# A mixture-of-experts dispatch on one core: the first group's last store in two pieces, and a load that waits for the first of them

## The chip, the cores and the metric

The kernel runs on one core of a Trainium2 chip. The metric is the device time of one execution in microseconds; three runs of the kernel before took 239.73, 239.82 and 239.9 us, so the median is 239.82 us.

## The reference

16384 tokens each have 512 numbers (`x`) and 8 router logits. For each token the two largest softmax probabilities are taken and divided by their sum, and the token's row is written twice, once scaled by each of the two weights, the smaller one first.

```python
logits_max = np.max(router_logits, axis=-1, keepdims=True)
probs = np.exp(router_logits - logits_max)
probs = probs / np.sum(probs, axis=-1, keepdims=True)
topk_indices = np.argsort(probs, axis=-1)[..., -k:]
topk_probs = np.take_along_axis(probs, topk_indices, axis=-1)
topk_probs = topk_probs / np.sum(topk_probs, axis=-1, keepdims=True)
x_expanded = x[:, :, np.newaxis, :].repeat(k, axis=2)
return (x_expanded * topk_probs[..., np.newaxis]).astype(np.float32)
```

Everything is float32. `x` is 33.6 MB, the logits 0.5 MB, and the output, with two rows for each token, 67.1 MB.

## The kernel before

The weights of the two chosen experts depend only on the difference of the two largest logits, so `top2_weights` finds these two with a small tree of maxima and minima on VectorE (lines 26 to 36) and gets both weights from two sigmoids on ScalarE (lines 37 and 38). They land in the tile `WA`.

The tokens are worked in two groups of 8192. In a group each of the 128 partitions holds 64 consecutive tokens, called rows below. A group has two loads of 32 rows each (line 118), into rows 0 to 31 and 32 to 63 of the tile `xs`, which both groups share. It then has four steps of 16 rows. Each step multiplies 16 rows by their two weights, which makes 32 output rows, and stores them (lines 131 to 159). The output goes in turn to the tile `osp` (steps 1 and 3) and back over rows of `xs` that have been used up: step 2 writes rows 0 to 31 of `xs`, step 4 rows 32 to 63. The product is a `tensor_tensor` on VectorE (line 147); of each group's first step a few rows go to ScalarE (line 140).

Every load and store of `x` and of the output is one transfer of 128 partitions x 16384 float32, so 64 KB for a partition and 8.4 MB in all. All transfers are issued by the SP engine, in program order (`tc.keep_in_program_order`), on one hardware queue. The order is: first load, logits, second load, four stores of the first group; third and fourth load; four stores of the second group. A transfer whose data is not ready, or whose target is still in use, holds up SP and all issues behind it.

Around the place of the change the order is this. The first group's second store (rows 0 to 31 of `xs`) must have landed before the second group's first load may overwrite those rows. The first group's last store reads rows 32 to 63 of `xs`, and the second group's second load, which overwrites them, waits for its landing. The second group's first load has nothing to do with the last store's data: it is issued right behind it and stands behind it in the queue. After that, the second group's first multiplication (line 147, into `osp`) waits for that load, and the second group's first store (line 158) waits for the multiplication.

Of the kernel before, what the change touches and what calls it, by code (L numbers as in the profile page):

```python
# [1 line left out]

# [4 lines left out]

F32 = mybir.dt.float32
ALU = mybir.AluOpType
ACTF = mybir.ActivationFunctionType  # L10
P = 128


def top2_weights(nc, WA, dlt, room, logits, E):

    tt = nc.vector.tensor_tensor
    hi, lo, n = None, None, E  # L20
    while n > 1:
        n //= 2
        if hi is None:
            a, b = logits[:, :, 0:n], logits[:, :, n : 2 * n]
            nhi, nlo = room(n), b
            tt(nhi, a, b, op=ALU.max)  # L26
            tt(nlo, a, b, op=ALU.min)  # L27
        else:
            a, b = hi[:, :, 0:n], hi[:, :, n : 2 * n]
            nhi, nlo, tmp = room(n), room(n), room(n)  # L30
            tt(tmp, lo[:, :, 0:n], lo[:, :, n : 2 * n], op=ALU.max)  # L31
            tt(nlo, a, b, op=ALU.min)  # L32
            tt(nlo, nlo, tmp, op=ALU.max)  # L33
            tt(nhi, a, b, op=ALU.max)  # L34
        hi, lo = nhi, nlo
    tt(dlt, hi[:, :, 0], lo[:, :, 0], op=ALU.subtract)  # L36
    nc.scalar.activation(WA[:, :, 0], dlt, ACTF.Sigmoid, scale=-1.0)  # L37
    nc.scalar.activation(WA[:, :, 1], dlt, ACTF.Sigmoid, scale=1.0)  # L38

GROUPS = [64, 64]

LOADS = [[32, 32], [32, 32]]
BASE = [0, 0]

STORES = [
    [(0, 16, "osp", 2), (16, 16, "xs", 0), (32, 16, "osp", 0), (48, 16, "xs", 32)],
    [(0, 16, "osp", 2), (16, 16, "xs", 0), (32, 16, "osp", 0), (48, 16, "xs", 32)],
]  # L50

L = 18

FREE = [2, 2]

ACT_ROWS = [5, 1]


@with_exitstack
def kernel(  # L60
    ctx: ExitStack,
    tc: tile.TileContext,
    x: bass.AP,
    router_logits: bass.AP,
    k: bass.AP,
    out: bass.AP,
):
    nc = tc.nc
    B, S, D = x.shape
    E = router_logits.shape[-1]  # L70
    N = B * S
    assert int(k) == 2 and E == 8 and N == P * sum(GROUPS)
    M = N // P

    x_v, o_v = [], []
    t0 = 0
    for n in GROUPS:
        t1 = t0 + P * n
        x_v.append(
            x.rearrange("b s d -> (b s) d")[t0:t1].rearrange("(p m) d -> p m d", p=P)  # L80
        )
        o_v.append(
            out.rearrange("b s k d -> (b s) k d")[t0:t1].rearrange(
                "(p m) k d -> p m k d", p=P
            )
        )
        t0 = t1

    wpool = ctx.enter_context(tc.tile_pool(name="wpool", bufs=1))
    xs = wpool.tile([P, max(GROUPS), D], F32)  # L90
    osp = wpool.tile([P, L, 2, D], F32)
    WA = wpool.tile([P, M, 2], F32)
    dlt = wpool.tile([P, M], F32)


    flat = osp.rearrange("p l k d -> p (l k d)")
    taken = [0]

    def room(n):
        o = taken[0]  # L100
        taken[0] += M * n
        return flat[:, o : o + M * n].rearrange("p (m n) -> p m n", n=n)

    logits = room(E)

    def place(where, at, n):

        if where == "osp":
            return osp[:, at : at + n]
        return xs[:, at : at + 2 * n, :].rearrange("p (r k) d -> p r k d", k=2)  # L110

    m0 = 0
    stores = []
    for g, G in enumerate(GROUPS):
        x0, r = BASE[g], 0
        for n in LOADS[g]:

            load = nc.sync.dma_start(xs[:, x0 + r : x0 + r + n, :], x_v[g][:, r : r + n, :])  # L118
            tc.keep_in_program_order(load)
            r += n  # L120
            if g == 0 and r == 32:
                n0 = GROUPS[0]
                assert GROUPS[1] == n0
                both = router_logits.rearrange("b s e -> (b s) e").rearrange(
                    "(g p m) e -> p g (m e)", g=2, p=P
                )
                at = logits.rearrange("p (g m) e -> p g (m e)", g=2)
                tc.keep_in_program_order(nc.sync.dma_start(at, both))
                top2_weights(nc, WA, dlt, room, logits, E)
        assert r == G  # L130
        for r, n, where, at in STORES[g]:
            og = place(where, at, n)

            again = where == "osp" and at == 0 and r > 0
            cuts = [0, FREE[g], n] if again else [0, n]
            if r == 0:
                cuts = [0, n - ACT_ROWS[g]]
                for j in range(n - ACT_ROWS[g], n):
                    for k2 in range(2):
                        nc.scalar.activation(  # L140
                            og[:, j, k2, :],
                            xs[:, x0 + r + j, :],
                            ACTF.Copy,
                            scale=WA[:, m0 + r + j, k2 : k2 + 1],
                        )
            for a, b in zip(cuts, cuts[1:]):
                nc.vector.tensor_tensor(  # L147
                    og[:, a:b],
                    xs[:, x0 + r + a : x0 + r + b, :]
                    .unsqueeze(2)  # L150
                    .to_broadcast([P, b - a, 2, D]),
                    WA[:, m0 + r + a : m0 + r + b, :]
                    .unsqueeze(3)
                    .to_broadcast([P, b - a, 2, D]),
                    op=ALU.mult,
                )

            stores.append(nc.sync.dma_start(o_v[g][:, r : r + n], og))  # L158
            tc.keep_in_program_order(stores[-1])
        m0 += G  # L160


# [1 line left out]
_INS = ['x', 'router_logits', 'k']  # L164
_OUTS = [((16, 1024, 2, 512), 'float32')]

_NUMBERS = {'k': 2}


# [26 lines left out]
```

## Time and profile before

The profile is that of one execution, which took 239.97 us; its span, from the first instruction to the last, is 238.2 us.

| What | Value |
|---|---|
| median of 3 runs | 239.82 us |
| the profiled execution | 239.97 us |
| its span | 238.2 us |
| ScalarE (ACT) busy | 9.3 us |
| GpSimd (POOL) busy | 0.2 us |
| mean rate of the transfers | 425 GB/s |
| read from and written to device memory | 34.08 MB and 67.11 MB |

How to read it: an engine's busy time counts its instructions and not its waits. The DMA row divides the span into 40 equal slices (5.96 us each) and gives the mean busy share of the 16 DMA engines in tenths. The chain of waits starts at the last instruction and goes back, at each step, to whatever released it; shown in order of time, each piece has its start, its length and what it was. `SPq` is SP's issuing of a transfer, and a piece that begins with `DMA` runs from the issue of a transfer to its landing, that is, until its data are in place and the semaphore that others wait for has been raised. Such a piece includes the time the transfer stood in the queue behind others.

### The profile page before, as it was taken

The page shows a single profiled execution, that of the slowest core. Times are in us where ns is not written, and L with a number is a line of the kernel's source. Part 1 is how long each engine was busy: PE and PEld are TensorE (multiplying, and loading weights), DVE is VectorE, ACT ScalarE, POOL GpSimd, SP SyncE. Part 2 cuts the span into 40 slices and gives each one's busy share as a digit, 9 for nine tenths or more (in the row PEclk, how much of TensorE's full clock was granted, in tenths as well). Part 3 has the DMA queues.
Part 4 walks back from the last instruction along what each step waited for, and adds up shares of the span by engine and source line. Part 5 has one row for each costly group of instructions (what it writes and reads, how often), then busy time and mean ns, then how long its engine had stood idle before and what let it go on. Part 6 is the DMA issues. An engine that isn't in the chain of part 4 may idle for free.

```text
span 238.2 us, 110 instructions
## 1 busy us (share of the span) xinstructions
DVE 135.4 (57%) x21; ACT 9.3 (4%) x15; POOL 0.2 (0%) x4
## 2 busy tenths in 40 slices
DVE  0000899999599999000000039999958999950000
ACT  2000370000000000000000020000000000000000
POOL 0000000000000000000000000000000000000000
DMA  9899898989999998989899998989898989899894
GB/s 352 363 517 440 352 528 352 528 352 484 396 440 440 396 484 352 528 352 528 352 484 396 396 484 352 528 352 517 363 517 363 517 363 495 385 462 418 374 506 176
DMA packets 2000, 101.19 MB, mean 425 GB/s; under 512 B 208, under 2 KB 208, under 8 KB 464
## 3 DMA queue, kind: packets, MB, share of 16 engines
q1 hardware_dynamic: 2000, 101.19, 98.6%
HBM read 34.08 MB, written 67.11 MB: 425 GB/s over the span
## 4 chain that ended last, share of the span: by engine, by line
DMA 47%; DVE 41%; issue 0%; SPq 0%; ACT 0%; DVEq 0%
DVE osp L147 24%; DMA xs<-in_x_dram 19%; DMA out_dram<-osp 19%; DVE xs L147 14%; DMA osp<-in_router_logits_dram 10%; DVE osp L26 0%; DVE osp L27 0%; DVE osp L33 0%; DVE osp L34 0%; DVE osp L32 0%; DVE osp L31 0%; SPq L118 0%; SPq L158 0%; ACT WA L38 0%; DVE dlt L36 0%
## 5 line engine op out<-in xcount | busy, mean ns | idle before, releaser
L147 DVE TENSOR_TENSOR osp<-xs,WA 128x2048 f32<-128x2048 f32 (+3 forms) x6 | 62.8, 10468 | 52.1 <-DMA xs<-in_x_dram 45.6
L147 DVE TENSOR_TENSOR xs<-xs,WA 128x16384 f32<-128x16384 f32 x4 | 68.9, 17225 | 0.3
L26 DVE TENSOR_TENSOR osp<-osp 128x512 f32<-128x512 f32 x1 | 0.7, 693 | 23.8 <-DMA osp<-in_router_logits_dram 23.8
L140 ACT ACTIVATE osp<-xs,WA 128x512 f32<-128x512 f32 x12 | 7.6, 707 | 106.1 <-DMA xs<-in_x_dram 106.1
L37 ACT ACTIVATE WA<-dlt 128x128 f32<-128x128 f32 x1 | 0.3, 315 | 25.8 <-DVE dlt L36 25.8
L37 ACT ACT_TABLE_LOAD x1 | 1.3, 1283 | 0.7 <-PEq L177 0.7
L27 DVE TENSOR_TENSOR osp<-osp 128x512 f32<-128x512 f32 x1 | 0.7, 691 | 0.0
L32 DVE TENSOR_TENSOR osp<-osp 128x256 f32<-128x256 f32 (+1 forms) x2 | 0.7, 352 | 0.0
L34 DVE TENSOR_TENSOR osp<-osp 128x256 f32<-128x256 f32 (+1 forms) x2 | 0.7, 352 | 0.0
L31 DVE TENSOR_TENSOR osp<-osp 128x256 f32<-128x256 f32 (+1 forms) x2 | 0.7, 351 | 0.0
L33 DVE TENSOR_TENSOR osp<-osp 128x256 f32<-128x256 f32 (+1 forms) x2 | 0.7, 350 | 0.0
L36 DVE TENSOR_TENSOR dlt<-osp 128x128 f32<-128x128 f32 x1 | 0.3, 293 | 0.0
L38 ACT ACTIVATE WA<-dlt 128x128 f32<-128x128 f32 x1 | 0.3, 297 | 0.0
L177 POOL MEMSET const-bfloat16-1.0<- 128x1 bf16 x1 | 0.1, 101 | 0.0
L177 POOL MEMSET const-uint8-127<- 128x1 uint8 x1 | 0.1, 101 | 0.0
L177 POOL MEMSET const-float32-0.0<- 128x1 f32 x1 | 0.1, 98 | 0.2 <-issue 0.2
L177 POOL MEMSET const-float32-1.0<- 128x1 f32 x1 | 0.1, 98 | 0.0
## 6 DMA issues: line engine op xcount, KB each, us to landing
osp<-in_router_logits_dram SPq DMA_DIRECT2D x1, 512.0 KB, 22.7
xs<-in_x_dram SPq DMA_DIRECT2D x4, 40.3
out_dram<-osp SPq DMA_DIRECT2D x4, 23.0
out_dram<-xs SPq DMA_DIRECT2D x4, 25.0
```

The lines of the kernel that those rows point to most:

```text
L26: tt(nhi, a, b, op=ALU.max)
L27: tt(nlo, a, b, op=ALU.min)
L31: tt(tmp, lo[:, :, 0:n], lo[:, :, n : 2 * n], op=ALU.max)
L32: tt(nlo, a, b, op=ALU.min)
L33: tt(nlo, nlo, tmp, op=ALU.max)
L34: tt(nhi, a, b, op=ALU.max)
L36: tt(dlt, hi[:, :, 0], lo[:, :, 0], op=ALU.subtract)
L37: nc.scalar.activation(WA[:, :, 0], dlt, ACTF.Sigmoid, scale=-1.0)
L38: nc.scalar.activation(WA[:, :, 1], dlt, ACTF.Sigmoid, scale=1.0)
L140: nc.scalar.activation(og[:, j, k2, :], xs[:, x0 + r + j, :], ACTF.Copy, scale=WA[:, m0 + r + j, k2 : k2 + 1],)
L147: nc.vector.tensor_tensor(og[:, a:b], xs[:, x0 + r + a : x0 + r + b, :] .unsqueeze(2) .to_broadcast([P, b - a, 2, D]), WA[:, m0 + r + a : ...
L177: nc = _bacc.Bacc("TRN2", target_bir_lowering=False, num_devices=1)
```

## The change

The last store of the first group is issued as two transfers, of partitions 0 to 111 and of partitions 112 to 127, one right after the other. The list `stores` then has one more entry, so that when the second group's first load is issued, `stores[-2]` is the one of 112 partitions. This load gets a wait of its own for that store's landing; the second group's second load, which overwrites the data of both, waits for the 16 partitions' landing, too. The instructions of the compute engines and their order are the same as before; SP has one issue more.

```diff
@@ -116,6 +116,15 @@
         for n in LOADS[g]:
 
             load = nc.sync.dma_start(xs[:, x0 + r : x0 + r + n, :], x_v[g][:, r : r + n, :])
+            if g == 1 and r == 0:
+                tc.add_manual_dep(
+                    load.ins,
+                    stores[-2].ins.name,
+                    mybir.DependencyInfo(
+                        mybir.DependencyClass.Sync, mybir.DependencyReason.DATA
+                    ),
+                    reason="begin when the store ahead of the last has landed",
+                )
             tc.keep_in_program_order(load)
             r += n
             if g == 0 and r == 32:
@@ -155,8 +164,10 @@
                     op=ALU.mult,
                 )
 
-            stores.append(nc.sync.dma_start(o_v[g][:, r : r + n], og))
-            tc.keep_in_program_order(stores[-1])
+            last = g == 0 and r + n == G
+            for p0, p1 in [(0, P - 16), (P - 16, P)] if last else [(0, P)]:
+                stores.append(nc.sync.dma_start(o_v[g][p0:p1, r : r + n], og[p0:p1]))
+                tc.keep_in_program_order(stores[-1])
         m0 += G
```

## The prediction

> **What bounds the kernel now.** I began with the page: its span, the busy row of the engines, the two DMA rows and the queue.
>
> ```profile
> span 238.2 us, 110 instructions
> DVE 135.4 (57%) x21; ACT 9.3 (4%) x15; POOL 0.2 (0%) x4
> DMA  9899898989999998989899998989898989899894
> DMA packets 2000, 101.19 MB, mean 425 GB/s; under 512 B 208, under 2 KB 208, under 8 KB 464
> q1 hardware_dynamic: 2000, 101.19, 98.6%
> ```
>
> The compute engines are idle for 43% of the span or more, while the 16 DMA engines are busy for 98.6% of it and the DMA row has no empty slice. This kernel is a stream of transfers, and only a gap in the stream, or a slower packet, can move its time. The packets say how the stream is built: 2000 less 464 small ones leaves 1536 large ones; over the 12 transfers of x and out that is 128 each, one per partition, or 8 on each of 16 engines (64 KB apiece, since a transfer is 128 x 16384 float32).
>
> Next the chain of waits in order of time, for where the stream sits around the edit.
>
> ```profile
> 40.30 22.22 DMA out_dram<-osp
> ...
> 94.92 0.33 SPq L158
> 95.26 0.05 issue
> 95.31 45.13 DMA xs<-in_x_dram
> 140.44 0.03 issue
> ...
> 140.53 16.17 DVE osp L147
> ...
> 156.76 22.46 DMA out_dram<-osp
> ```
>
> The second piece is the edit's place. The first group's last store (I call the stores S1 to S8 and the x loads L1 to L4) is S4, issued at 94.92. L3 is issued at 95.31, right behind it in the same queue, and lands 45.13 us later, at 140.44. It spends most of that time behind S3 and S4. Then the timeline and the issue table, asked for one issue at a time, give the landings.
>
> ```profile
> 57.56 0.34 SPq L158 DMA_DIRECT2D out_dram<-xs  x1
> ...
> 77.67 0.33 SPq L158 DMA_DIRECT2D out_dram<-osp  x1
> ...
> 120.88 0.34 SPq L118 DMA_DIRECT2D xs<-in_x_dram  x1
> ```
>
> ```profile
> out_dram<-xs SPq DMA_DIRECT2D x1, 24.3
> ...
> out_dram<-osp SPq DMA_DIRECT2D x1, 23.5
> ...
> out_dram<-xs SPq DMA_DIRECT2D x1, 25.9
> ...
> xs<-in_x_dram SPq DMA_DIRECT2D x1, 39.0
> ```
>
> The last column is us from issue to landing; the rows are S2, S3, S4 and L4. S1 landed at 40.30 + 22.22 = 62.52, S2 at 81.86, S3 at 77.67 + 23.5 = 101.17, S4 at 94.92 + 25.9 = 120.82, L4 at 159.9. So a store takes (101.17 - 62.52) / 2 = 19.33 us in the undisturbed stream, and one partition's packet 19.33 / 8 = 2.42 us. L4 took 159.9 - 140.44 = 19.46. Loads and stores go at one pace, so its limit is neither the read nor the write of the far memory but what both use: the 16 engines, or the way from each engine into on-chip memory. The trace cannot part these two, and the forecast hangs on which it is.
>
> From S3's landing to L3's is 140.44 - 101.17 = 39.27 us against 2 x 19.33 = 38.66: the switch from storing to loading loses 0.6 us. That is all there is to win here.
>
> **The change, part by part.** One more issue on SP: 0.33 us (the S4 row above), at about 95.3. S3 occupies the engines until 101.17, so some 6 us of queued work hide it; without that cover it would cost its 0.33 us. The small packets are 13 issues x 16 = 208 under 512 B, so 16 more come with the new store; S1 to S3 ran at 19.33 us with theirs included, and I cost them at nothing.
>
> The added wait. L3 no longer stands in the queue from 95.31 but is issued when the 112 partitions have landed. Behind it on SP stand L4, which waited for S4 anyway, and S5, which is not due before 156.76.
>
> ```profile
> SPq L118 <- DMA out_dram<-xs: 24.3, 1, 24.3
> ...
> DVE osp L147 <- DMA xs<-in_x_dram: 45.6, 1, 45.6
> ```
>
> The first row is L4's wait for S4; it now begins later and costs nothing by itself. The second is VectorE waiting for L3, and whatever delays L3 is added to it in full. What a load needs when nothing is queued ahead is seen once, in L1:
>
> ```profile
> xs<-in_x_dram SPq DMA_DIRECT2D x1, 21.8
> ```
>
> That is 21.8 - 19.33 = 2.5 us of start and landing beyond the bare transfer. The cover for it is the 16-partition store, one packet on each engine. Spread evenly at the known pace that is 2.42 us: the wait would be hidden to within 0.1 us. If the cover were gone, the wait would cost up to 2.5 us.
>
> The split store is the expensive part, and the trace has no transfer on fewer than 128 partitions. The nearest in size is the logits load:
>
> ```profile
> 1.15 22.67 DMA osp<-in_router_logits_dram
> ```
>
> It landed at 23.82, 1.3 us behind L1 (0.72 + 21.8 = 22.52), which is 0.5 MB at about the stream's pace; but it too covers all 128 partitions. So I bound the 16 partitions (1.05 MB) from both ends. Low: all 16 engines move one packet each at full pace, 2.42 us. High: in a full store two engines' ways carry 16 partitions, 8 each, and if the 16 neighbours have only two such ways, 19.33 us. Between lie 8 ways (4.83 us) and 4 ways (9.67 us). A ladder in powers of two has no row that decides it. By size it is nearest to the low end; but the identical pace of loads and stores lets the limit be the way into on-chip memory, and then it goes with the partitions that a way serves, 8 each in a full transfer. I take 4 ways, 9.67 us, and keep both ends.
>
> The Trainium skill's page "SBUF — State Buffer", section "Door 1: The DMA port swizzle", says that partitions reach on-chip memory by 16 ports of 8 partitions, that a run of 16 neighbours reaches only 4 of them, and that such a run was measured at 104 GB/s. No row here shows it; by that figure the 16 partitions would take an estimated 10.1 us, and with the full 112-partition loss below the time would be 249.9.
>
> The 112 partitions are 7 per engine. If nothing is shared they end after 7 x 2.42 = 16.92 us. If ways belong to 8 partitions each, most ways still have all 8 to deliver, so the slowest engines end nearer to 8 x 2.42 = 19.33 us. Then the 16 follow. The sum from S3's landing is 16.92 + 9.67 = 26.59 at the low end and 19.33 + 9.67 = 29.0 at the high end, against 19.33 for the whole store before: +7.26 to +9.67 us. Seven-packet runs of 16 engines cannot fall evenly on ways of eight, so I take three quarters of the way up: +9.07 us.
>
> Does anything downstream swallow it? L3, L4, S5 and all later transfers follow on the late engines without a gap. S5 was ready at 156.76, 3.1 us before L4 landed at 159.9, and both move with L3. Engines that finish S4 early run ahead and then wait for S5, but the late ones set every landing. So the shift reaches the end whole. The profiled execution took 239.97 us, of which 238.2 is span and 1.77 lies around it: 239.97 + 9.07 = 249.04. It is 0.15 above the median of the runs, 239.82, so I predict 248.9.
>
> **The rivals.**
> 1. *Even spread: not slower.* The limit is the engine, not the way, so the 16 partitions take 2.42 us. The place is L3's start. The 112 land 16.92 us after S3 at 118.09, and an idle-queue load needs 21.8 us: 139.9, against 140.44 before, thus 0.5 us faster if the store-to-load loss goes (239.3). If that loss stays, it is about 0.1 us the other way (239.9). It decides from 4.83 us downwards. For it speak the logits row and the cover of 2.42 against a need of 2.5; against it, only that a limit shared by loads and stores may as well be the way.
> 2. *Eight ways.* The 16 partitions take 4.83 us and the 112 lose nothing: +2.42, 242.2. The rows speak neither for nor against it.
> 3. *Fewer engines, or crossing ways throughout.* The split may put 8 partitions on an engine, so that the 112 use 14 engines and the 16 then load two of these again: 2 x 19.33 against 19.33, or +19.3 (259.1). Or all 16 engines walk neighbouring partitions in step in the 112 as well, at a quarter pace: 7 x 9.67 = 67.7 us for them, +50 or more. Against both: nothing in the trace but the even 8 packets per engine of full transfers. The Trainium skill's page "DMA: Bandwidth & Descriptors", section "Why a DMA increments its semaphore by 16 and not by 1", says that the largest count up to 16 that divides the partitions is used, which is 16 engines for 112 and for 16; no row here shows a partial transfer, and by it the first half of this rival would fall and its 259.1 with it.
> 4. *The change does not do what it says.* L3 already stands behind S4 in the queue, so a wait that only repeats this order moves nothing by itself; that is rival 1 with 239.8, and I count it there.
>
> **How the numbers follow.** The forecast has 0.70, rival 1 with 4 has 0.18, rival 2 0.06, rival 3 0.06. About 0.2% (0.5 us) is what a measurement of this kernel can tell from no change. Of rival 1's 0.18 I put 0.08 on a gain beyond that and 0.10 inside; slower is 0.70 + 0.06 + 0.06 = 0.82. The forecast's own range is +7.26 to +9.67, or 247.1 to 249.5, and 251.0 with a costlier restart of L3 (up to 2.5 us of idle start, of which 1.5 is allowed). The range that holds 8 in 10 takes in rival 2 and the neutral part of rival 1: 239.4 to 251.0. Left out are the gain beyond that end and rival 3.
>
> **What would show it.** L3's issue moves from 95.31 to when the 112 land: about 118 by rival 1, 118 to 121 by the forecast. The 16 partitions land some 29 us after S3 (near 130) by the forecast and near 120.5 by rival 1. L3 lands near 149.5 or near 140. VectorE's wait for L3 grows from 45.6 to about 55, and the DMA row shows a dent below 9 behind slice 20 (119 us). The spacing of S5 to S8 stays 19.33 us in every case. The forecast is wrong if the 16 land within 5 us of the 112, or if the delay of L3 is gone by S5's landing.

## The result, and the profile after

The changed kernel takes 250.24 us (median of 4 runs, 250.2 to 250.55) against 239.8 us before. The ratio is 1.0438, with a 95% interval of 1.0425 to 1.0451: 10.4 us slower. The prediction was 248.9 us.

The page of the changed kernel, its span, the busy row of the engines, the DMA rows and the queue:

```profile
span 248.5 us, 111 instructions
DVE 135.4 (54%) x21; ACT 9.2 (4%) x15; POOL 0.2 (0%) x4
...
DMA  8989989999898999979998999979899898989984
GB/s 338 475 369 422 496 348 506 401 443 496 348 496 348 506 401 443 433 306 411 200 317 359 433 422 464 390 317 464 380 485 475 369 485 380 464 380 485 464 380 190
DMA packets 2016, 101.19 MB, mean 407 GB/s; under 512 B 224, under 2 KB 224, under 8 KB 480
q1 hardware_dynamic: 2016, 101.19, 97.4%
```

VectorE's busy time and the bytes are unchanged, and there are 16 more small packets, those of the added store. The DMA engines still look busy (97.4%, and no slice below 7 except the last). The GB/s row shows what happened: in five slices between 106 and 137 us it reads 306, 411, 200, 317 and 359, on the mean 319, against a mean of 425 over the whole span before. A packet that takes long counts as busy for as long as it takes, so for a slow transfer the rate must be read, not the busy share.

The chain of waits in order of time, around the edit:

```profile
95.34 27.81 DMA out_dram<-xs
123.16 0.02 issue
123.17 0.02 SPq L118
123.19 0.03 issue
123.22 27.75 DMA xs<-in_x_dram
150.97 0.02 issue
150.99 16.17 DVE osp L156
...
167.23 22.40 DMA out_dram<-osp
```

Where the chain of before went straight from S4's issue into L3, it now goes through the landing of the 112 partitions at 123.16, and L3 is issued only then. L3 needs 27.75 us from there, 6 us more than the 21.8 us of a load with nothing ahead of it, because the 16 partitions stand before it. The table of stretches from landing to landing shows how long; its columns are the stretch, its length, the engines' busy times, the granted clock, the DMA share and GB/s. The last two book a packet whole in the stretch where it starts, so a share can pass 1. First the kernel before, S2 and S3, then S4, then L3:

```profile
62.52:101.17 38.65, 32.32 (x2) 0.00 (x0) 0.00 (x0) 1.00 1.00 434
101.17:120.82 19.65, 0.00 (x0) 0.00 (x0) 0.00 (x0) 1.00 1.01 427
120.82:140.44 19.62, 0.00 (x0) 0.00 (x0) 0.00 (x0) 1.00 0.99 428
```

And the changed kernel, with S4 in its two pieces:

```profile
62.94:101.54 38.60, 32.32 (x2) 0.00 (x0) 0.00 (x0) 1.00 1.01 435
101.54:123.16 21.62, 0.00 (x0) 0.00 (x0) 0.00 (x0) 1.00 1.04 340
123.16:129.75 6.59, 0.00 (x0) 0.00 (x0) 0.00 (x0) 1.00 0.64 219
129.75:150.97 21.22, 0.00 (x0) 0.00 (x0) 0.00 (x0) 1.00 1.00 426
```

S4 takes 21.62 + 6.59 = 28.2 us in place of 19.65, which is 8.6 us of the loss; L3 behind it takes 21.22 in place of 19.62, another 1.6. The profiled execution also reached S3's landing 0.4 us later (101.54 against 101.17), ahead of the edit. Together that is 150.97 - 140.44 = 10.5 us, less some 0.2 us regained behind L3, which makes the 248.5 - 238.2 = 10.3 us between the spans. Last, the waits of VectorE for L3:

```profile
DVE osp L156 <- DMA xs<-in_x_dram: 55.7, 1, 55.7
...
DVE osp L156 <- DMA out_dram<-osp: 5.8, 2, 3.0
```

The first grew from 45.6 to 55.7; the second, the wait of the second group for its own stores, did not move. Nothing downstream gave anything back.

### The profile page after: what moved, and what is told of

Same layout as the page of the kernel before. It is cut to its first block, busy times and chain, and to the rows that moved or that the text cites. A ratio compares the mean times of both kernels' runs of the same rounds, so it can differ in the third digit from the quotient of the medians.

```text
span 248.5 us, 111 instructions
## 1 busy us (share of the span) xinstructions
DVE 135.4 (54%) x21; ACT 9.2 (4%) x15; POOL 0.2 (0%) x4
## 3 DMA queue, kind: packets, MB, share of 16 engines
q1 hardware_dynamic: 2016, 101.19, 97.4%
## 4 chain that ended last, share of the span: by engine, by line
DMA 50%; DVE 39%; issue 0%; SPq 0%; ACT 0%
DVE osp L156 23%; DMA out_dram<-osp 18%; DVE xs L156 14%; DMA out_dram<-xs 11%; DMA xs<-in_x_dram 11%; DMA osp<-in_router_logits_dram 9%; DVE osp L26 0%; DVE osp L27 0%; DVE osp L33 0%; DVE osp L34 0%; DVE osp L32 0%; DVE osp L31 0%; SPq L118 0%; ACT WA L38 0%; DVE dlt L36 0%
## 5 line engine op out<-in xcount | busy, mean ns | idle before, releaser
L156 DVE TENSOR_TENSOR osp<-xs,WA 128x2048 f32<-128x2048 f32 (+3 forms) x6 | 62.8, 10467 | 62.0 <-DMA xs<-in_x_dram 55.7
```

What stands on the lines that cost most here:

```text
L156: nc.vector.tensor_tensor(og[:, a:b], xs[:, x0 + r + a : x0 + r + b, :] .unsqueeze(2) .to_broadcast([P, b - a, 2, D]), WA[:, m0 + r + a : ...
```

## The experiments

The theory: ways into on-chip memory serve fixed sets of partitions, a transfer over neighbouring partitions reaches only some of them, and engines that meet on one way share it; the added wait is a small matter. The main rival: the wait, or splitting at all, is the cost.

**The split without the wait**

```diff
-            if g == 1 and r == 0:
-                tc.add_manual_dep(load.ins, stores[-2].ins.name,
...
```

> The store of the first group's last step goes out as 112 and 16 partitions, without the added wait. Theory (the narrow pieces share ways into on-chip memory, and the split alone is the cost): the 16 partitions land about 28 us after the store before, as in the changed kernel, and the third load follows on each engine without a pause; 248 to 249 us, that is 1 to 2 us under the changed kernel, because the early engines no longer wait. Rival (the wait is the cost): within 0.5 us of the kernel before, 239.3 to 240.3.

It took 249.55 us, ratio 1.0405 (1.0391 to 1.042): 9.6 us of the 10.4. The stretches of this kernel: the 112, the 16, L3.

```profile
101.20:123.96 22.76, 0.00 (x0) 0.00 (x0) 0.00 (x0) 1.00 1.04 340
123.96:129.88 5.92, 0.00 (x0) 0.00 (x0) 0.00 (x0) 1.00 0.64 255
129.88:150.48 20.60, 0.00 (x0) 0.00 (x0) 0.00 (x0) 1.00 1.02 439
```

The two pieces take 28.7 us with no wait at all, so the split is the cost, and the rival falls. The expectation was 0.5 to 1.5 us low: the two pieces take 28.7 us and not 28, and L3 takes 20.6 us here, too, and not 19.6. It had also put this kernel 1 to 2 us under the changed one; it is 0.7 us under it.

**The wait without the split**

```diff
+            if g == 1 and r == 0:
+                tc.add_manual_dep(load.ins, stores[-1].ins.name,
...
```

> The last store stays whole, and the third load waits for its landing. Theory (the wait costs the start of a load on an idle queue, 2.5 us, less the 0.6 us that the switch from storing to loading loses now): the load lands about 1.9 us later, 241.7 us, range 241.2 to 242.3. Rival (the wait is the greater part of the 10 us): 246 or more.

It took 242.03 us, ratio 1.0087 (1.0073 to 1.0101). The chain of this kernel:

```profile
95.01 25.47 DMA out_dram<-xs
120.48 0.02 issue
120.49 0.02 SPq L118
120.51 0.03 issue
120.54 21.78 DMA xs<-in_x_dram
142.32 0.03 issue
```

An uncovered wait costs what L1's row said: the load needs 21.78 us from its issue instead of a transfer's 19.33. With no load queued behind it, S4 lands at 120.48, 19.3 us after S3. Both halves of the prediction's reckoning of the wait are seen here, and 2.1 us is far from 10.4. The two costs do not add up (9.6 + 2.1 = 11.7) because in the changed kernel most of the wait lies beside the 16 partitions' slow packets: a load's start takes 21.78 - 19.33 = 2.45 us, and the 16 run for another 6.59 us when L3 is issued.

**The same split by rows, with and without the wait**

```diff
-            for p0, p1 in [(0, P - 16), (P - 16, P)] if last else [(0, P)]:
-                stores.append(nc.sync.dma_start(o_v[g][p0:p1, r : r + n], og[p0:p1]))
+            for j0, j1 in [(0, n - 2), (n - 2, n)] if last else [(0, n)]:
+                stores.append(nc.sync.dma_start(o_v[g][:, r + j0 : r + j1], og[:, j0:j1]))
```

> The last store is split by rows instead of partitions: all 128 partitions x 14 rows, then all 128 x 2 rows; the same shares of the bytes (7/8 and 1/8), and the third load waits for the first piece. Theory (only the partitions' choice is at fault): no shared ways, the two pieces take 16.9 and 2.4 us, the wait is covered; 239.2 to 240.1 us. Rival (any split with a wait in it costs): the 10 us of the changed kernel or a good part of them, 243 or more.

With the wait it took 240.21 us, ratio 1.0014 (1.0005 to 1.0023). The chain:

```profile
95.08 23.07 DMA out_dram<-xs
118.14 0.02 issue
118.16 0.02 SPq L118
118.18 0.03 issue
118.21 22.45 DMA xs<-in_x_dram
140.65 0.02 issue
```

The seven eighths land at 118.14, where rival 1 had put them, and L3 at 140.65, 0.2 us later than before. The same bytes in the same shares with the same wait cost 0.3 us instead of 10.4, so what costs is the choice of partitions. The time is 0.1 us above the upper end expected.

> The same split by rows, 14 and 2, without the added wait. Theory: nothing but one more issue and smaller packets at the end; within 0.3 us of the kernel before, 239.5 to 240.1. If the wait of the row split removes the 0.6 us that the switch from storing to loading loses, this one is 0.3 to 0.6 us slower than the row split with the wait; otherwise the two are equal within 0.2 us.

Without the wait it took 239.91 us, ratio 0.9995 (0.9986 to 1.0004), no change. The wait in the row split gained nothing: with it the kernel takes 0.3 us more, where the expectation had allowed 0.2 between two equal ones.

**The 16 partitions alone**

This diff and those that follow show the lines of the store; where an expectation says that no wait is added, the lines of the wait are left out as well.

```diff
-            for p0, p1 in [(0, P - 16), (P - 16, P)] if last else [(0, P)]:
+            for p0, p1 in [(P - 16, P)] if last else [(0, P)]:
```

> Of the first group's last store only partitions 112 to 127 are stored; the other 112 are left out, and no wait is added. This prices the 16 neighbouring partitions alone: the time is that of the kernel before, 239.9, less 19.33 us for a whole store, plus their own time. Full pace on 16 engines (2.42 us): 223.0. Eight ways (4.83 us): 225.4. Four ways (9.67 us, the theory): 230.2, up to 231.5 with the slower start of the load behind it. Two ways (19.33 us): 239.9.

It took 229.91 us against 239.59 for the kernel before, measured beside it, so the 16 partitions cost 229.91 - (239.59 - 19.33) = 9.65 us. Its stretch from S3's landing to the landing of the 16, and two shorter ones cut so that the first holds just the starts of the store's packets:

```profile
101.20:110.59 9.39, 0.00 (x0) 0.00 (x0) 0.00 (x0) 1.00 0.26 112
...
100.23:101.20 0.97, 0.00 (x0) 0.00 (x0) 0.00 (x0) 1.00 9.75 1081
101.20:109.40 8.20, 0.00 (x0) 0.00 (x0) 0.00 (x0) 1.00 0.00 0
```

The first: 1.05 MB in 9.39 us, 112 GB/s against 435, a quarter, as with four ways. The others show how. All 16 packets start within 0.97 us, and none follows for 8.2 us; their time, 9.75 x 0.97 us = 9.46 us for each of the 16 engines, is 3.9 times the 2.42 us of a packet before. The records do not name the engine of a packet, but 16 packets are under way at once, as many as in the undisturbed stream. So it is not that few engines work: all 16 are at it, each at a quarter of its pace.

**Every eighth partition in place of the 16 neighbours**

```diff
-            for p0, p1 in [(P - 16, P)] if last else [(0, P)]:
-                stores.append(nc.sync.dma_start(o_v[g][p0:p1, r : r + n], og[p0:p1]))
+            for step in [8] if last else [1]:
+                stores.append(nc.sync.dma_start(o_v[g][::step, r : r + n], og[::step]))
```

> The same with every eighth partition (0, 8, ... 120) in place of 112 to 127: again 16 partitions, the other 112 left out, and no wait added. Theory (ways belong to fixed sets of neighbouring partitions, so spread partitions reach more of them): 8 ways, 4.83 us, 225.4, and in any case at least 3 us under the run with 16 neighbours. Rival (the price goes by the number of partitions or the size of the transfer, wherever they lie): equal to that run within 1 us.

It took 225.58 us. The stretch of the 16 partitions:

```profile
101.18:105.46 4.28, 0.00 (x0) 0.00 (x0) 0.00 (x0) 1.00 0.71 245
```

As many bytes from as many partitions go at 245 GB/s, more than twice as fast, because they lie apart. So neither the number of partitions nor the size sets the price. The 4.28 us are less than the 4.83 us of eight ways; why is open.

**Which side of the transfer decides**

The two sets of partitions differ on both sides of the transfer, in on-chip memory and in the output. Two runs cross them:

```diff
-                stores.append(nc.sync.dma_start(o_v[g][::step, r : r + n], og[::step]))
+                stores.append(nc.sync.dma_start(o_v[g][P - 16 :, r : r + n], og[::step]))
```

(for this one store), and the reverse, `o_v[g][::8, r : r + n]` from `og[P - 16 :]`.

> Again only 16 partitions of the first group's last store: read from every eighth partition of on-chip memory, but written to the places in the output that belong to partitions 112 to 127; the rest of that store is left out, no wait is added. If the place in on-chip memory sets the pace (theory): as with every eighth partition to its own place, 225.6, the store landing some 4.3 us after the store before. If the spacing of the places in device memory sets it (rival): as with the 16 neighbours, 229.9 and 9.4 us.

> The reverse: read from partitions 112 to 127, written to the places that belong to every eighth partition; the rest of that store is left out, no wait is added. If the place in on-chip memory sets the pace (theory): 229.9, the store landing some 9.4 us after the store before. If the spacing in device memory sets it (rival): 225.6 and 4.3 us.

Read from every eighth partition it took 225.71 us, read from 112 to 127 it took 229.94 us, wherever they were written. The issue tables, S3's and S4's rows with us to landing; the first kernel issued them at 77.82 and 95.08, the second at 78.03 and 95.29:

```profile
out_dram<-osp SPq DMA_DIRECT2D x1, 23.4
...
out_dram<-xs SPq DMA_DIRECT2D x1, 10.2
```

```profile
out_dram<-osp SPq DMA_DIRECT2D x1, 23.4
...
out_dram<-xs SPq DMA_DIRECT2D x1, 15.5
```

S4 lands 4.1 us after S3 in the first (105.28 and 101.22) and 9.4 us after it in the second (110.79 and 101.43). The place in on-chip memory sets the pace; the spacing in device memory does not.

**Two halves**

```diff
-            for p0, p1 in [(0, P - 16), (P - 16, P)] if last else [(0, P)]:
+            for p0, p1 in [(0, P // 2), (P // 2, P)] if last else [(0, P)]:
```

> The store whole in two halves, partitions 0 to 63 and 64 to 127, no added wait. Theory (each half reaches only half of the ways, so both run at half pace): 2 x 19.33 in place of 19.33, 259.2, up to 260.5 with the slower start of the load. Rival (a fixed price for a second, narrower transfer, as the split in 112 and 16 showed it): 249.5. Rival (only pieces of few partitions are slow): 239.9.

It took 260.73 us, ratio 1.0878 (1.0846 to 1.0909). The stretches of the two halves:

```profile
101.17:120.71 19.54, 0.00 (x0) 0.00 (x0) 0.00 (x0) 1.00 1.01 215
120.71:140.78 20.07, 0.00 (x0) 0.00 (x0) 0.00 (x0) 1.00 0.88 206
```

Each half goes at half the rate. This is no fixed price of a second transfer, and it is worse than 112 and 16.

**The small piece first**

```diff
-            for p0, p1 in [(0, P - 16), (P - 16, P)] if last else [(0, P)]:
+            for p0, p1 in [(0, 16), (16, P)] if last else [(0, P)]:
```

> The same two pieces with the small one first, partitions 0 to 15 and then 16 to 127, no added wait. Theory (engines that meet on one way share it; with 112 first, the last engines' tail overlaps with the 16): the 16 run alone at quarter pace for 9.67 us, then the 112 take about 22.4 us alone: 32.1 in place of 19.33, 252.7, up to 254 with the slower start of the load. Rival (the price is the 16 partitions' 9.67 us alone and does not depend on order): 249.5 as with 112 first.

It took 252.03 us, ratio 1.0515 (1.0476 to 1.0554). The stretches of the 16 and the 112:

```profile
101.20:110.69 9.49, 0.00 (x0) 0.00 (x0) 0.00 (x0) 1.00 0.30 110
110.69:132.25 21.56, 0.00 (x0) 0.00 (x0) 0.00 (x0) 1.00 0.99 365
```

Order matters by 2.5 us against the split with 112 first. The 112 take 21.6 us here and in the changed kernel, and 22.8 us in the split without the wait. The 16 take 9.5 us when they run alone but only about 6 us beyond the 112 when they come second. The changed kernel's stretch of the 112, cut in two, shows why:

```profile
101.54:118.75 17.21, 0.00 (x0) 0.00 (x0) 0.00 (x0) 1.00 0.97 362
118.75:123.16 4.41, 0.00 (x0) 0.00 (x0) 0.00 (x0) 1.00 1.31 253
```

At 65.5 KB each, 95 packets begin in the first part and 17 in the second. With the 16 that had begun before 101.54 these are all 128 packets of both pieces, begun before the 112 have landed. The 95 take 2.81 us each on the mean (0.97 x 16 x 17.21 / 95), the 17 take 5.4 us (1.31 x 16 x 4.41 / 17), a pace at which most of them must be packets of the 16 partitions. So an engine begins on the 16 when its own seven packets are done, while others still work on the 112. The measured time is 0.7 us below the 252.7 expected.

**What was meant to be won.** From S3's to L3's landing the kernel before loses 0.6 us against two undisturbed transfers. Two more kernels tried for it: the row split in 12 and 4, whose second piece covers the load's start with a margin, and the whole store with L3 waiting for the landing of S3, so that it stands in the queue for a shorter time.

```diff
-            for j0, j1 in [(0, n - 2), (n - 2, n)] if last else [(0, n)]:
+            for j0, j1 in [(0, n - 4), (n - 4, n)] if last else [(0, n)]:
```

> All 128 partitions in both pieces, 12 rows and then 4, and the third load waits for the 12. The cover is 4.83 us instead of 2.42, more than the 2.5 us that a load needs to start. Theory (with 14 and 2 rows the cover was some 0.4 us short, since the load landed 22.45 us after its wait ended; a covered wait wins nothing else): the time of the kernel before within 0.3 us, 239.5 to 240.1. Rival (the wait keeps the load's reads away from the store and so saves the 0.6 us of the switch): 239.2 to 239.4.

```diff
-                tc.add_manual_dep(load.ins, stores[-1].ins.name,
+                tc.add_manual_dep(load.ins, stores[-2].ins.name,
```

(against the wait without the split).

> The last store whole, and the third load waits for the landing of the store ahead of it, so that it enters the queue at about 101.2 instead of 95.3, still 19 us before its turn. Theory (only what happens when the queue turns from store to load matters, not how early the load was queued): no change, within 0.3 us of the kernel before. Rival (a load that stands long in the queue slows the store ahead): 0.4 to 0.7 us faster, 239.1 to 239.5.

They took 240.05 us, ratio 1.0006 (0.9995 to 1.0016), and 239.91 us, ratio 0.9999 (0.999 to 1.0007). Neither differs from the kernel before. The chains have L3 at

```profile
115.69 24.61 DMA xs<-in_x_dram
140.29 0.02 issue
```

in the first and at

```profile
101.42 39.28 DMA xs<-in_x_dram
140.70 0.03 issue
```

in the second, against 140.44 before. A covered wait wins at most 0.15 us at L3, and nothing of it is left at the end. No kernel here that stores the whole output beats the one before.

## Why the prediction was right, point by point

**What bounds the kernel.** The stream of transfers, as said: every change of S4's or L3's landing reached the end, within 0.3 us.

**The added issue and the small packets** at nothing: right as far as it can be seen, for the row split without a wait has both and equals the kernel before.

**The wait.** Its uncovered price was put at 2.5 us, less 0.6 of the switch; measured alone it was 2.1 us. With the row split's last eighth as cover, 0.3 us stayed of it: L3 landed 22.45 us after its issue, so the cover was a little short, as 2.42 against 2.5 had warned.

**The 16 partitions** at four ways and 9.67 us, chosen between 2.42 and 19.33: measured alone 9.65 us by the time and 9.39 by the landings. The choice had no row to decide it and could have gone wrong; the runs with every eighth partition and with crossed places show that its reason holds. The rule of the Trainium skill that was weighed beside it, in "SBUF — State Buffer", section "Door 1: The DMA port swizzle", agrees: its four of 16 ports would give the quarter of the pace that was measured, and 112 GB/s here stands against its 104, for a transfer of the same 1 MiB.

**The 112 partitions** were put between 16.92 and 19.33 us, by the argument that a way with all its eight partitions still has eight packets to deliver. They took 21.6 us, and 22.8 us in the split without the wait, so this bound was too low. Eight packets is what a way needs if it is never idle. The engines were busy all the while (a DMA share of 0.97 in the first 17.21 us, at 362 GB/s), but their packets took 2.81 us in place of 2.42. That this is so because engines meet on one way while other ways stand idle is argued, not shown. The error was covered by another: the 16 were added whole, but they took only some 6 us beyond the 112. The sum from S3's landing came out within 0.2 us, 28.4 predicted (19.33 + 9.07) and 28.2 measured, and so close a hit is luck: each of its two terms was about 3 us off, in opposite directions.

**L3 behind the split** is the term that was mis-sized. It stood at nothing in the sum and at up to 1.5 us in the range; it measured 1.6 us (21.22 against 19.62). Without the wait it is 1.0 us (20.60), so the greater part belongs to the uneven split. The time is lost in L3's first packets, as two more stretches of the changed kernel show:

```profile
129.75:131.00 1.25, 0.00 (x0) 0.00 (x0) 0.00 (x0) 1.00 1.43 472
133.00:135.40 2.40, 0.00 (x0) 0.00 (x0) 0.00 (x0) 1.00 0.95 410
```

The 9 packets that begin just after the 16 have landed take 3.2 us each (1.43 x 16 x 1.25 / 9), the 15 that begin from 133.00 on take 2.4 us (0.95 x 16 x 2.40 / 15); why the first are slow is open. What the wait costs in the changed kernel is not settled either. The two kernels' times differ by 0.7 us, but in the profiled executions only 0.15 of it lies between S3's and L3's landing (49.43 us against 49.28) and 0.34 ahead of the edit (S3 at 101.54 against 101.20). L3's 1.6 us are why the result lies 1.3 us above the prediction; the forecast's own range with its restart, up to 251.0, holds it.

**The rivals.** Even spread fell with the first run that priced the 16 alone, and so did eight ways and fewer engines: 229.9 us against 223.0, 225.4 and 239.9. Neighbours that meet throughout the 112 as well, at a quarter of the pace, would have taken 67.7 us for them; they took 21.6. Whether the engine or its way into on-chip memory sets the pace was left open, since full transfers cannot part the two; the crossed runs settle it for the way, for with as many packets of the same size in both, and all 16 under way at once in the run with the neighbours alone, the pace went by the place in on-chip memory alone. Which partitions share a way is not shown beyond the sets that were run.

**What was to be seen.** The 16 landed 28.2 us after S3 (29 said) and 6.6 us behind the 112, not far above the 5 us that were to prove the forecast wrong. L3 landed at 150.97 (149.5 said), VectorE's wait grew to 55.7 (55 said), S5 to S8 kept their spacing. L3 was issued at 123.2, later than the 118 to 121 said, for the reason given at the 112. A dent in the DMA row was wrong: the row stays at 7 to 9, and only the GB/s row shows it.

## What to carry to other kernels

In a kernel bound by its transfers, split a transfer along its rows and keep all 128 partitions in every piece: without a wait, the split by rows cost nothing that could be measured, the split by partitions 9.6 us. When a profile of full-width transfers has no row for a narrow one, bound it by the share of the ways that its partitions can reach and not by its bytes, and add the collisions of the wider piece. And a saturated queue already hides a load's start: in these runs a wait that orders what the queue orders cost 2.1 us without cover and 0.3 us with a short one; a covered one cost nothing, and none gained anything at the end.

## What the runs showed of the hardware that was not expected

The engines do not recover from an uneven split at once: the load behind it took 20.3 us (behind the halves) to 21.2 us where 19.6 is usual, and 20.6 us in the run with every eighth partition (from that store's landing at 105.46 to the load's at 126.10), but not behind the 16 neighbours alone (19.66 us from 110.59 to 130.25). Why it is slower in some of these and not in others was not settled.

A store with no load queued behind it landed 0.3 us sooner (120.48 against 120.82, in profiles whose S3 landed within 0.05 us of each other), and yet no placing of the wait kept that gain. The last 16 packets of S4 are where it lies: in the kernel before, those that begin from 117.00 to 117.62 took 2.72 us each (a share of 4.38 x 0.62 us), in the run with the wait alone those from 117.00 to 118.00 took 2.42 us (2.42 x 1.00).
